# Expert feed-forward: experts sorted by token count, three of them with 64 slots, and a share of the weight splitting on GpSimd

## Chip, cores and metric

The kernel runs on one core of a Trainium2 chip. The metric is the device time of one execution in microseconds (us); the number quoted is the median over the runs.

## What is computed

The reference is a two-layer encoder trunk on 256 tokens of width 1024. The change touches the last stage, the second layer's channel mixer, in which each token goes to the best two of eight experts:

```python
logits = h @ router_w + router_b
top_v, top_i = lax.top_k(logits, 2)
probs = softmax(top_v)
for e in range(8):
    out += combine[..., e:e+1] * ((silu(h @ w1[e]) * (h @ w3[e])) @ w2[e])
```

Here `w1[e]` and `w3[e]` are 1024 x 3584 and `w2[e]` is 3584 x 1024, all in fp32: 44 MB an expert, 352 MB in all.

## The kernel before

**Precision.** TensorE multiplies in a reduced-precision fp32 form (`F32R`), so each operand is split into a high and a low part: ScalarE writes `hi` as a copy in that form, VectorE then writes `lo = x - hi` (`split`, lines 271 to 273). A product takes three matmuls, `hi*hi`, `hi*lo` and `lo*hi` (`mm3`, lines 275 to 280).

**Tokens.** Every expert has 128 slots. `tokens` makes, for two experts at a time, a 0/1 matrix `sel` that puts the chosen tokens in the slots, gathers their `h` by matmul, and splits it into the parts in `hg` (in one of three places, named `hhi`, `hlo` or `hg` in the trace). `selT` and `wsl` bring the result back with the router's weight. A second pass over all experts runs only if an expert has over 128 tokens.

**Blocks.** An expert's 3584 hidden columns are cut into seven blocks of 512 (`f`), so there are 56 blocks. In a block, `up` makes `ph` for `w1` and for `w3`: eight chunks of the 1024 inputs, three matmuls each with the token part stationary and 512 weight columns moving, so 48 matmuls. Then ScalarE takes Silu of the first (line 1739) and VectorE multiplies by the second and by `wsl` (line 1740, tile `ea`). `turned` transposes `ea` by four TensorE instructions into `aT` and splits it into `eahi` and `ealo`; `down` adds 24 matmuls into the two accumulators `py`. `up` of a block stands ahead of `down` of the block before it.

**Weights.** A block reads six tiles of 1 MiB (two each of `w1`, `w3`, `w2`) into 14 raw buffers: ten named `er`, and the places `ey`, `hg` and `x`, of which four are filled at the start and two stay in use. SyncE issues all of them in order (line 163), each when its buffer is free. `Stream.splits` turns each tile into two pieces of 1024 columns, `eh` (ScalarE) and `el` (VectorE), in four buffers each, asked for three pieces ahead of their use. Each engine's order comes from a scheduler that lays the program out when it is built.

Of the kernel before, what the change touches and what calls it, by code (L numbers as in the profile page):

```python
# [35 lines left out]
T = 256  # L36
# [9 lines left out]
CAP = 128  # L46
# [4 lines left out]
def _consts():  # L51
# [24 lines left out]
    late["slots"] = np.broadcast_to(p, (128, 128))  # L76
    out = []
# [52 lines left out]
class Stream:  # L130
# [19 lines left out]
    def load(self, upto):  # L150
        while self.loaded < min(upto, len(self.tiles)):
            t = self.tiles[self.loaded]
            k, m = self.loaded - self.bufs, len(self.more)
            if k >= m:
                k = (k - m) % (self.bufs + self.keep) - self.bufs + m - self.keep
            if k >= m - self.keep or 0 <= k == self.loaded - self.bufs:
                raw = self.more[k]()
            else:
                raw = self.pool.tile([128, self.raw], F32, name=self.name + "r", tag=self.name + "r", bufs=self.bufs)
            dst = raw[:, :t[1]]  # L160
            if len(t[0].shape) == 3:
                dst = dst.rearrange("p (a b) -> p a b", a=t[0].shape[1])
            self.k.nc.sync.dma_start(dst, t[0])
            t[2] = raw
            self.loaded += 1
# [6 lines left out]
    def splits(self, upto):  # L172
        nc = self.k.nc
        while self.split < min(upto, len(self.units)):
# [3 lines left out]
            if not whole:  # L178
# [70 lines left out]
FFN_SPAN = 6, 42  # L249
MM = 0.109  # L250


class K:
# [17 lines left out]
    def split(self, hi, lo, src):  # L271
        self.nc.scalar.activation(hi, src, AF.Copy)  # L272
        self.nc.vector.tensor_sub(lo, src, hi.bitcast(F32))  # L273
# [1257 lines left out]
    def moe(self, l):  # L1531
# [44 lines left out]
        pe.matmul(ps[:, 8:16], self.c("before"), ind[:, 1, :], start=False, stop=True)  # L1576
        pos = t28("place")
        v.tensor_copy(pos.rearrange("p a e -> p (a e)"), ps[:, :16])
        comb = t28("comb")
        mxc = mk.tile([1, 1], I32, name="mxc")  # L1580

        def weights():
# [19 lines left out]
            over = mk.tile([1, 8], F32, name="over")  # L1602
            ps = self.pg("cnt")
            pe.matmul(ps[0:32, 0:8], self.c("ones")[:, 0:32], ind[:, 0, :], start=True, stop=False)
            pe.matmul(ps[0:32, 0:8], self.c("ones")[:, 0:32], ind[:, 1, :], start=False, stop=True)
            v.tensor_copy(over, ps[0:1, 0:8])
            v.tensor_reduce(mxc, over, axis=AX.X, op=OP.max)

        self.todo, self.pending, self.rsh = [], [weights], rsh
        self.comb, self.ind, self.pos, self.gate2, self.shift2 = comb, ind, pos, mod[:, 16:24], mod[:, 0:8]  # L1610
        with ExitStack() as s2:
            self.pshh = s2.enter_context(tc.tile_pool(name="pshh", bufs=2, space=PSUM))
            self.psy = s2.enter_context(tc.tile_pool(name="psy", bufs=1, space=PSUM))
            self.experts(ws)
            self.final()
            cnt = nc.values_load(mxc, min_val=0, max_val=256)
            with tc.If(cnt > CAP):
                self.pos = t28("place2")
                v.tensor_scalar(self.pos, pos, float(-CAP), None, op0=OP.add)
                self.experts(self.expert_stream())  # L1620
                self.final()
# [8 lines left out]
    def tokens(self, e0, first=False):  # L1630
# [7 lines left out]
        hg = [self.room((e0 + i) % 3).rearrange("p (i k s) -> p i k s", i=2, k=KB) for i in range(2)]  # L1638
        flat = [sel[:, tt].rearrange("p e s -> p (e s)") for tt in range(2)]

        def find(i):
            e = e0 + i
            for tt in range(2):
                v.tensor_scalar(sel[:, tt, i, :], self.c("slots"), self.pos[:, tt, e:e + 1], self.ind[:, tt, e:e + 1],
                                op0=OP.is_equal, op1=OP.mult)
# [4 lines left out]
        def norms():  # L1650
            ps = self.pg("rsb")[:, :256]
            for n in range(4):
                pe.matmul(ps, self.rsh[:, n // 2, n % 2:n % 2 + 1].to_broadcast([128, 128]), flat[n % 2], start=n == 0, stop=n == 3)
            act.activation(rsb, ps, AF.Copy)

        def gather(kb):
            if kb % 2 == 0:
                pk[0] = self.psy.tile([128, 512], F32, name="py0", tag=f"py{kb // 4}") if kb // 2 % 2 and first else self.pg("hg")
            ps, shift = pk[0][:, kb % 2 * T:kb % 2 * T + T], self.shift2[:, kb:kb + 1]
# [3 lines left out]
            v.tensor_mul(ps, ps, rsb)  # L1663
            for i in range(2):
                hi, lo, x = hg[i][:, 0, kb, :], hg[i][:, 1, kb, :], ps[:, i * 128:i * 128 + 128]
# [3 lines left out]
        def back(i):  # L1669
            e = e0 + i  # L1670
# [9 lines left out]
        self.todo += [lambda i=i: find(i) for i in range(2)]  # L1680
# [3 lines left out]
        self.todo += self.pending + [lambda i=i: back(i) for i in range(2)]  # L1684
        self.pending = []
        return hg, selT, wsl
# [7 lines left out]
    def expert_stream(self, more=(), keep=0):  # L1694
        I, nf = self.I, DFE // 512
        ws = Stream(self, self.es, "e", 2048, RAW, 1024, 4, 3, self.eq, more, keep)
        seq = [(e, f) for e in range(NE) for f in range(nf)]
        for x, y in zip(seq + [None], [None] + seq):
            if x:
                e, f = x  # L1700
                for w in ("moe_w1", "moe_w3"):
                    for k0 in (0, 4):
                        ws.add((w, e, f), I[w][e, k0 * 128:k0 * 128 + 512, f * 512:f * 512 + 512]
                               .rearrange("(k p) n -> p k n", p=128), 2048)
            if y:
                e, f = y
                for k0 in (0, 2):
                    r = f * 512 + k0 * 128
                    ap = I["moe_w2"][e, r:r + 256, :]
                    if y == seq[-1]:  # L1710
                        ap = I["moe_w2"][e, f * 512:f * 512 + 512, k0 * 256:k0 * 256 + 512]
                    ws.add(("moe_w2", e, f), ap.rearrange("(k p) n -> p k n", p=128), 2048)
        return ws

    def experts(self, ws):
# [5 lines left out]
        def up(e, f, hg, wsl, behind):  # L1721
            i = e % 2
            hps = []
            for w in ("moe_w1", "moe_w3"):
                if behind and w == "moe_w3":
                    behind[2] = turned(behind[2])
                ps = self.pshh.tile([128, 512], F32, name="ph", tag="p" + w)
                for k0 in range(0, 8, 2):
# [11 lines left out]
            v.scalar_tensor_tensor(a, a, wsl[:, i:i + 1], hps[1], op0=OP.mult, op1=OP.mult)  # L1740
            return a

        def turned(a, spare=False):
            pt = self.pg("aT")
            for k in range(4):
# [10 lines left out]
        def down(e, f, aT, py, selT, then=None):  # L1756
            ahi, alo = aT
            ends, last = f == nf - 1, e == NE - 1 and f == nf - 1
            for p in range(4):
                whi, wlo = ws.take(("moe_w2", e, f), 2)  # L1760
                for j in range(2):
                    c, kk = (p // 2, p % 2 * 2 + j) if last else (j, p)
                    self.mm3(py[c], ahi[:, kk * 128:kk * 128 + 128], alo[:, kk * 128:kk * 128 + 128],
                             whi[:, j, :], wlo[:, j, :], start=f == 0 and kk == 0, stop=ends and kk == 3)
                if then and p == 0:
                    then[2] = turned(then[2], True)
# [14 lines left out]
            elif ends:  # L1781
                for c in range(2):
                    self.todo.append(lambda c=c: self.split(y[:, 0, c, :], y[:, 1, c, :], py[c]))
# [3 lines left out]
        def back(e, kk, y, selT):  # L1787
            ps = self.pg("sct").rearrange("p (a t) -> p a t", a=2)
            for a in range(2):
                n = (kk + a) % 4 * 128  # L1790
                for j in range(2):
                    pe.matmul(ps[:, a, :], y[:, j, kk // 4, n:n + 128], selT[:, e % 2, :], start=a == 0 and j == 0, stop=j == 1,
# [12 lines left out]
        behind, nxt = None, self.tokens(0, True)  # L1805
        for e in range(NE):
            if e % 2 == 0:
                self.step(len(self.todo) if e else 0)
                hg, selT, wsl = nxt
            py = [self.psy.tile([128, 512], F32, name=f"py{c}", tag=f"py{c}") for c in range(2)]  # L1810
            for f in range(nf):
                a = up(e, f, hg, wsl, behind)
                now = [e, f, a, py, selT]
                if behind:
                    down(*behind, now if e == NE - 1 and f == nf - 1 else None)
                behind = now
                if e % 2 and f == nf - 4 and e < NE - 1:
                    nxt = self.tokens(e + 1)
        down(*behind)
# [71 lines left out]

def layout(inputs):
# [34 lines left out]
        "moe_w1": n["moe_w1"][0],  # L1927
        "moe_w3": n["moe_w3"][0],
        "moe_w2": n["moe_w2"][0],
# [19 lines left out]
```

## Time and profile before

| | |
|---|---|
| runs | 1762.18, 1765.52 (median), 1766.88 us |
| the profiled execution | 1767.88 us, of which its span (first to last instruction) 1766.1 us |
| TensorE / VectorE / ScalarE / GpSimd busy | 1686.6 / 1530.3 / 1188.5 / 6.6 us |
| granted TensorE clock, mean | 0.985 |

A "busy" TensorE is one with a matmul in flight; the ends of matmuls are modelled and they overlap, so its pace is read from the distance between starts. Times in the sections below count from the start of the span.

### The profile page before, as it was taken

The page shows a single profiled execution, that of the slowest core. Times are in us where ns is not written, and L with a number is a line of the kernel's source. Part 1 is how long each engine was busy: PE and PEld are TensorE (multiplying, and loading weights), DVE is VectorE, ACT ScalarE, POOL GpSimd, SP SyncE. Part 2 cuts the span into 40 slices and gives each one's busy share as a digit, 9 for nine tenths or more (in the row PEclk, how much of TensorE's full clock was granted, in tenths as well). Part 3 has the DMA queues.
Part 4 walks back from the last instruction along what each step waited for, and adds up shares of the span by engine and source line. Part 5 has one row for each costly group of instructions (what it writes and reads, how often), then busy time and mean ns, then how long its engine had stood idle before and what let it go on. Part 6 is the DMA issues. An engine that isn't in the chain of part 4 may idle for free.

```text
span 1766.1 us, 29679 instructions
## 1 busy us (share of the span) xinstructions
PE 1686.6 (95%) x11192; PEld 1466.2 (83%) x11192; DVE 1530.3 (87%) x2386; ACT 1188.5 (67%) x1774; POOL 6.6 (0%) x19
## 2 busy tenths in 40 slices
PE   5887999999989999899999999999999999999996
PEld 4776999999988899788888888888888888888885
DVE  7887788888869888689999998999999999999996
ACT  3645556555565655478878777777777787777775
POOL 0000000000000000000000000000000000000000
PEclk9999999999989999899999999999999999999998
DMA  8724465888733657979999999999999999999980
GB/s 283 251 92 157 153 208 190 294 288 289 249 98 125 204 185 230 345 277 366 379 344 343 355 342 366 370 351 331 352 361 372 346 365 337 347 373 367 353 304 26
DMA packets 193812, 501.93 MB, mean 284 GB/s; under 512 B 11498, under 2 KB 13162, under 8 KB 193660
## 3 DMA queue, kind: packets, MB, share of 16 engines
q1 hardware_dynamic: 192652, 498.50, 79.8%
q8 instruction: 89, 1.46, 0.3%
q10 hardware_dynamic: 720, 1.42, 0.2%
q14 instruction: 63, 0.52, 0.1%
q0 software_dynamic: 288, 0.03, 0.0%
HBM read 498.86 MB, written 1.05 MB: 283 GB/s over the span
## 4 chain that ended last, share of the span: by engine, by line
PE 77%; DVE 11%; DMA 7%; issue 3%; ACT 2%; SPq 0%; DVEq 0%; ACTq 0%
PE ph L279 10%; PE ph L278 10%; PE ph L280 10%; PE py L279 5%; PE py L280 5%; PE py L278 5%; PE pj L278 4%; PE pj L279 4%; PE pj L280 4%; DVE el L273 3%; DMA er<-in_moe_w_dram 3%; PE psh L278 2%; PE psh L279 2%; PE psh L280 2%; DVE wl L273 2%
## 5 line engine op out<-in xcount | busy, mean ns | idle before, releaser
L273 DVE TENSOR_TENSOR el<-er,eh 128x1024 fp32r<-128x1024 f32 x560 | 661.8, 1221 | 25.7 <-ACT eh L272 13.9
L272 ACT ACTIVATE eh<-er 128x1024 fp32r<-128x1024 f32 x560 | 580.9, 1059 | 104.0 <-PE ph L280 54.8
L272 ACT ACTIVATE wh<-wr 128x512 fp32r<-128x512 f32 (+1 forms) x366 | 223.0, 620 | 210.3 <-PE pj L279 61.5
L273 DVE TENSOR_TENSOR wl<-wr,wh 128x512 fp32r<-128x512 f32 (+1 forms) x366 | 242.8, 674 | 59.6 <-ACT wh L272 57.3
L278 PE MATMUL pj<-hhi,wh 128*128 128x256 f32 x704 | 206.6, 299 | 8.0 <-ACT hhi L400 7.3
L279 PE MATMUL pj<-hlo,wh 128*128 128x256 f32 x704 | 200.6, 287 | 0.6 <-DVE hlo L273 0.5
L280 PE MATMUL pj<-hhi,wl 128*128 128x256 f32 x704 | 200.5, 286 | 0.6 <-DVE wl L273 0.6
L279 PE MATMUL py<-el,eahi 128*128 128x512 f32 x440 | 175.1, 398 | 0.7
L280 PE MATMUL py<-eh,ealo 128*128 128x512 f32 x440 | 171.8, 391 | 0.0
L278 PEld LDWEIGHTS pj<-hhi,wh 128*128 128x128 f32 x704 | 134.5, 194 | 16.2 <-ACT hhi L400 8.9
L278 PE MATMUL py<-eh,eahi 128*128 128x512 f32 x440 | 146.4, 390 | 0.0
L279 PEld LDWEIGHTS pj<-hlo,wh 128*128 128x128 f32 x704 | 136.4, 194 | 2.8 <-issue 1.1
L280 PEld LDWEIGHTS pj<-hhi,wl 128*128 128x128 f32 x704 | 136.4, 194 | 1.9 <-DVE wl L273 1.1
L273 DVE TENSOR_TENSOR el<-x,eh 128x1024 fp32r<-128x1024 f32 x108 | 128.2, 1221 | 8.0 <-ACT eh L272 6.1
L278 PE MATMUL ph<-eh,hhi 128*128 128x512 f32 x336 | 133.6, 398 | 0.5 <-ACT hhi L1666 0.5
L278 PE MATMUL ph<-eh,hlo 128*128 128x512 f32 x336 | 133.2, 396 | 0.0
L279 PE MATMUL ph<-el,hhi 128*128 128x512 f32 x336 | 133.0, 396 | 0.1
L279 PE MATMUL ph<-el,hlo 128*128 128x512 f32 x336 | 132.9, 396 | 0.0
L280 PE MATMUL ph<-eh,hhi 128*128 128x512 f32 x336 | 131.9, 393 | 0.0
L280 PE MATMUL ph<-eh,hlo 128*128 128x512 f32 x336 | 131.8, 392 | 0.0
L272 ACT ACTIVATE eh<-x 128x1024 fp32r<-128x1024 f32 x108 | 111.6, 1057 | 14.2 <-PE ph L280 12.8
L279 PEld LDWEIGHTS py<-el,eahi 128*128 128x128 f32 x440 | 82.7, 188 | 19.8 <-DVE el L273 3.2
(413 smaller groups left out, 3389.7 us busy)
## 6 DMA issues: line engine op xcount, KB each, us to landing
er<-in_moe_w_dram SPq DMA_DIRECT2D x280, 1024.0 KB, 7.1
x<-in_moe_w_dram SPq DMA_DIRECT2D x54, 1024.0 KB, 7.1
wr<-in_ada_w_dram SPq DMA_DIRECT2D x64, 512.0 KB, 4.4
wr<-in_w_in_dram SPq DMA_DIRECT2D x52, 512.0 KB, 4.3
wr<-in_ffn_up_dram SPq DMA_DIRECT2D x44, 512.0 KB, 4.4
aw<-in_ada_w_dram SPq DMA_DIRECT2D x32, 512.0 KB, 4.8
wr<-in_ffn_w_dram SPq DMA_DIRECT2D x22, 512.0 KB, 4.7
wr<-in_w_o_dram SPq DMA_DIRECT2D x16, 512.0 KB, 4.6
```

What stands on the lines that cost most here:

```text
L272: self.nc.scalar.activation(hi, src, AF.Copy)
L273: self.nc.vector.tensor_sub(lo, src, hi.bitcast(F32))
L278: mm(out, whi, xhi, start=start, stop=False, skip_group_check=True)
L279: mm(out, whi, xlo, start=False, stop=False, skip_group_check=True)
L280: mm(out, wlo, xhi, start=False, stop=stop, skip_group_check=True)
```

## The change

1. **Order.** `arranged` counts the tokens of each expert on the chip, ranks the experts by it and sets which expert is worked on at which place: expert 0 first, then by turns one of the three with the fewest tokens (places 1, 3, 5, the set `SMALL`) and one of the others. The weights of places 1 to 7 are read from an address that SyncE takes from a register (`order`).
2. **Small experts.** They have 64 slots. The high part of `h` fills columns 0 to 63 of the stationary operand, the low part columns 64 to 127. A product then takes two matmuls, by `whi` and by `wlo`, and rows 0 to 63 and 64 to 127 of `ph` are added later: both `ph` are copied to SBUF (`ea`, `eb`), and eight matmuls by the constant `sum2` add and transpose them at once. Silu and the product follow on 128x256 (`ez`), and both parts go into one stationary operand for `down` (`ealo`), with `wsl` applied at the end (`weighed`).
3. **GpSimd.** For the small experts' weights, VectorE writes the first 640 columns of a piece of `el` and GpSimd the last 384 (`POOLED`).
4. **Weights in memory.** They are laid out so that each partition's 2048 elements of a tile lie together; before, they were four runs of 512 (`w1`, `w3`) or two of 1024 (`w2`).
5. **Groups.** `tokens` runs for places (0), (1, 2), (3, 4), (5, 6), (7) in place of pairs. A second pass over all experts runs if one has more tokens than its slots.

```diff
+SMALL = (1, 3, 5)
+PLACE = (0, 5, 1, 6, 2, 7, 3, 4)
+GROUPS = ((0,), (1, 2), (3, 4), (5, 6), (7,))
+POOLED = 384
...
+                elif self.aside(r):
+                    m = n - POOLED
+                    self.k.split(hi[:, :n], lo[:, :m], src, m)
+                    self.k.nc.gpsimd.tensor_sub(lo[:, m:n], src[:, m:], hi[:, m:n].bitcast(F32))
...
     def expert_stream(...):
-                        ws.add((w, e, f), I[w][e, k0 * 128:k0 * 128 + 512, f * 512:f * 512 + 512]
-                               .rearrange("(k p) n -> p k n", p=128), 2048)
+                at = lambda i=i: I[w][bass.ds(self.order(e), 1), f, i].rearrange("a p n -> (a p) n")
+                ws.add((w, e, f), at if e and sorted_ else I[w][e, f, i], 2048)
...
     up:
-                        self.mm3(ps, hg[i][:, 0, kb, :], hg[i][:, 1, kb, :], whi[:, k, :], wlo[:, k, :],
-                                 start=kb == 0, stop=kb == 7)
+                        if e in small:
+                            pe.matmul(ps, x[:, kb, :], whi[:, k, :], start=kb == 0, stop=False, skip_group_check=True)
+                            pe.matmul(ps, x[:, kb, :], wlo[:, k, :], start=False, stop=kb == 7, skip_group_check=True)
+                        else:
+                            self.mm3(ps, hi[:, kb, :], lo[:, kb, :], whi[:, k, :], wlo[:, k, :], start=kb == 0, stop=kb == 7)
...
+            if e in small:
+                b = self.ex.tile([128, 512], F32R, name="eb", tag="eahi", bufs=1).bitcast(F32)
+                v.tensor_copy(a, hps[0])
+                v.tensor_copy(b, hps[1])
+                return a, b
...
     turned:
+            if e in small:
+                for i in range(2):
+                    for k in range(4):
+                        o = i * 256 + k * 64
+                        pe.matmul(pt[:, o:o + 64], a[i][:, k * 128:k * 128 + 128], self.c("sum2"), start=True, stop=True)
+                z = self.work.tile([128, T], F32, name="ez", tag="sq", bufs=3)
+                tc.keep_in_program_order(act.activation(z, pt[:, :T], AF.Silu))
+                v.tensor_mul(z, z, pt[:, T:])
...
+                v.tensor_copy(t4[:, :, 0, :], z)
+                v.tensor_sub(t4[:, :, 1, :], z, t4[:, :, 0, :].bitcast(F32))
...
     down:
+                    if e in small:
+                        pe.matmul(py[c], aT[:, sl], whi[:, j, :], start=first, stop=False, skip_group_check=True)
+                        pe.matmul(py[c], aT[:, sl], wlo[:, j, :], start=False, stop=stop, skip_group_check=True)
...
-        behind, nxt = None, self.tokens(0, True)
+        behind, hg = None, self.tokens(GROUPS[0], small, True)
```

`arranged` is some 26 VectorE instructions on tiles of at most 64 columns and two matmuls.

**TensorE, inside `up`.** Before, one piece of the weights in the middle of an expert (two of the eight chunks) and the first row of the next; `eh` and `el` are the piece's parts, and a name in brackets is the engine whose result the instruction waits for:

```order
L278 MATMUL ph<-eh,hhi 128x512 [waits Activation_49]
L279 MATMUL ph<-el,hhi 128x512 [waits DVE_49]
L280 MATMUL ph<-eh,hhi 128x512
L278 MATMUL ph<-eh,hhi 128x512
L279 MATMUL ph<-el,hhi 128x512
L280 MATMUL ph<-eh,hhi 128x512
L278 MATMUL ph<-eh,hhi 128x512 [waits Activation_49]
```

After, the same place in a small expert (`hlo` holds the tokens here):

```order
L1814 MATMUL ph<-eh,hlo 128x512 [waits Activation_49]
L1815 MATMUL ph<-el,hlo 128x512 [waits DVE_49]
L1814 MATMUL ph<-eh,hlo 128x512
L1815 MATMUL ph<-el,hlo 128x512 [waits Pool_49]
L1814 MATMUL ph<-eh,hlo 128x512 [waits Activation_49]
```

A piece goes from six matmuls to four, and the last of the four, which reads the columns past 640, waits for GpSimd.

**VectorE.** Before, around the Silu's product of one block (a gather of tokens stands between here, on `hhi`):

```order
L273 TENSOR_TENSOR el<-er,eh 128x1024 [waits PE_49]
L1667 SCALAR_TENSOR_TENSOR hhi<-hg,mod_7670,hhi 128x128 [waits Activation_49] x2
L1740 SCALAR_TENSOR_TENSOR ea<-ea,wsl,ph 128x512 [waits Activation_49]
L273 TENSOR_TENSOR el<-er,eh 128x1024 [waits DMAHW1_49,PE_49]
L273 TENSOR_TENSOR el<-er,eh 128x1024 [waits Activation_49]
```

After, in a small expert, from the copy of one `ph` to the product of the block:

```order
L290 TENSOR_TENSOR el<-er,eh 128x640 [waits DMAHW1_49,Activation_49]
L290 TENSOR_TENSOR el<-er,eh 128x640 [waits Activation_49]
L290 TENSOR_TENSOR el<-er,eh 128x640 [waits DMAHW2_49,PE_49,Activation_49]
L290 TENSOR_TENSOR el<-er,eh 128x640 [waits PE_49,Activation_49]
L290 TENSOR_TENSOR el<-er,eh 128x640 [waits DMAHW3_49,PE_49,Activation_49]
L290 TENSOR_TENSOR el<-er,eh 128x640 [waits PE_49,Activation_49]
L1825 COPY ea<-ph 128x512 [waits PE_49]
L290 TENSOR_TENSOR el<-er,eh 128x640 [waits DMAHW4_49,Activation_49]
L1843 TENSOR_TENSOR ez<-ez,aT 128x256 [waits Activation_49]
L290 TENSOR_TENSOR el<-er,eh 128x640 [waits Activation_49]
L1846 CAST ealo<-ez 128x4x64 [waits DVE_49]
L1847 TENSOR_TENSOR ealo<-ez,ealo 128x4x64 [waits DVE_49]
```

Each `el` row is 640 columns wide in place of 1024, and between them stand the copies of `ph` and the three instructions that make `ez` and `ealo`.

**GpSimd, the same stretch.** Before there is nothing here. After, a row for each piece, on the tiles that VectorE's rows read and write:

```order
L199 TENSOR_TENSOR el<-er,eh 128x384 [waits DMAHW1_49,PE_49,Activation_49]
L199 TENSOR_TENSOR el<-er,eh 128x384 [waits PE_49,Activation_49]
L199 TENSOR_TENSOR el<-er,eh 128x384 [waits DMAHW2_49,PE_49,Activation_49]
L199 TENSOR_TENSOR el<-er,eh 128x384 [waits PE_49,Activation_49]
L199 TENSOR_TENSOR el<-er,eh 128x384 [waits DMAHW3_49,PE_49,Activation_49]
```

Both engines wait for ScalarE's `eh` of the piece.

## Rows read from the trace of the kernel before

**Rows 1.** The page, whole kernel: busy time by engine; 40 slices of 44 us.

```profile
PE 1686.6 (95%) x11192; PEld 1466.2 (83%) x11192; DVE 1530.3 (87%) x2386; ACT 1188.5 (67%) x1774; POOL 6.6 (0%) x19
...
PE   5887999999989999899999999999999999999996
DVE  7887788888869888689999998999999999999996
ACT  3645556555565655478878777777777787777775
...
PEclk9999999999989999899999999999999999999998
DMA  8724465888733657979999999999999999999980
GB/s 283 251 92 157 153 208 190 294 288 289 249 98 125 204 185 230 345 277 366 379 344 343 355 342 366 370 351 331 352 361 372 346 365 337 347 373 367 353 304 26
```

**Rows 2.** The page: what ended last, by engine.

```profile
PE 77%; DVE 11%; DMA 7%; issue 3%; ACT 2%; SPq 0%; DVEq 0%; ACTq 0%
```

**Rows 3.** Line 1739, the Silu of each block: count, first and last start.

```profile
L1739 ACT ACTIVATE ea<-ph x56: 577/579/601, 771.9 to 1733.3; 128x512 f32<-128x512 f32 x56
```

**Rows 4.** TensorE in order of time, one block: start, duration (us), instruction.

```profile
1052.56 0.39 PE L278 MATMUL ph<-eh,hg 128*128 128x512 f32 x1
1052.79 0.39 PE L279 MATMUL ph<-el,hg 128*128 128x512 f32 x1
...
1068.13 0.60 PE L1746 MATMUL aT<-cst,ea 128*128 128x128 f32 x4
1068.49 0.48 PE L279 MATMUL py<-el,eahi 128*128 128x512 f32 x1
1068.80 0.40 PE L280 MATMUL py<-eh,ealo 128*128 128x512 f32 x1
...
1069.50 0.39 PE L278 MATMUL ph<-eh,hg 128*128 128x512 f32 x1
```

**Rows 5.** Windows: that block, and all blocks: busy us by engine, clock, DMA.

```profile
core 0: us, PE busy (x) PEld busy (x) DVE busy (x) ACT busy (x) POOL busy (x), PEclk, DMA share, GB/s
1052.56:1069.50 16.94, 16.94 (x77) 13.88 (x76) 15.29 (x15) 13.23 (x15) 0.00 (x0) 1.00 1.01 376
772.00:1733.00 961.00, 960.05 (x4405) 787.59 (x4404) 889.17 (x924) 746.58 (x837) 0.00 (x0) 1.00 0.96 348
```

**Rows 6.** Groups by shape, 800 to 1700 us: busy, mean ns, idle before.

```profile
L273 DVE TENSOR_TENSOR el<-er,eh 128x1024 fp32r<-128x1024 f32 x513 | 606.3, 1221 | 23.4 <-ACT eh L272 12.0 <-DMA er<-in_moe_w_dram 0.2
L272 ACT ACTIVATE eh<-er 128x1024 fp32r<-128x1024 f32 x513 | 532.4, 1059 | 95.7 <-PE ph L280 48.0 <-PE py L280 38.4 <-DVE el L273 5.4
L1740 DVE SCALAR_TENSOR_TENSOR ea<-ea,wsl,ph 128x512 f32<-128x512 f32 x51 | 37.8, 742 | 0.1
L273 DVE TENSOR_TENSOR ealo<-aT,eahi 128x512 fp32r<-128x512 f32 x51 | 35.1, 689 | 29.8 <-ACT eahi L272 29.6
L272 ACT ACTIVATE eahi<-aT 128x512 fp32r<-128x512 f32 x51 | 30.4, 596 | 76.0 <-PE py L279 44.6 <-PE aT L1746 31.4
```

**Rows 7.** SyncE's queue, 800 to 1700 us: what its issues waited for.

```profile
SPq L163 <- DVE el L273: 693.3, 280, 4.1
```

**Rows 8.** Groups by shape, whole kernel: the nearest rows for new operations.

```profile
L273 DVE TENSOR_TENSOR wl<-wr,wh 128x512 fp32r<-128x512 f32 x348 | 235.7, 687 | 59.5 <-ACT wh L272 57.3 <-PE pj L280 0.6 <-issue 0.3
L1331 DVE COPY kT<-qkT 96x512 f32<-96x512 f32 x8 | 5.5, 682 | 0.1
L1663 DVE TENSOR_TENSOR hg<-hg,rsb 128x256 f32<-128x256 f32 x28 | 11.8, 427 | 3.7 <-PE hg L1661 3.4
L1301 DVE COPY k<-krot 128x512 f32<-128x512 f32 x2 | 0.8, 421 | 0.0
L273 DVE TENSOR_TENSOR falo<-fa,fahi 128x256 fp32r<-128x256 f32 x22 | 9.2, 418 | 0.0
L1674 ACT ACTIVATE selT<-selT 128x256 fp32r<-128x256 f32 x8 | 3.1, 382 | 1.8 <-PE selT L1673 1.8
```

**Rows 9.** All of GpSimd's groups that write a tile of size.

```profile
L987 POOL MEMSET f<- 128x512 f32 x2 | 1.1, 542 | 0.0
L985 POOL MEMSET f<- 128x256 f32 x2 | 0.7, 326 | 136.5 <-PE pj L280 136.5
```

**Rows 10.** DMA, 1040 to 1120 us in slices of 2 us; transfers into `er`.

```profile
GB/s 392 383 381 329 414 408 377 382 327 331 403 375 386 387 379 318 394 298 378 372 326 372 406 307 371 385 335 286 389 371 405 407 407 391 332 397 363 367 384 420
DMA packets 12650, 29.66 MB, mean 371 GB/s; under 512 B 450, under 2 KB 450, under 8 KB 12645
...
DMA to landing us min/median/max: 3.3/7.1/15.7
L163 SPq DMA_DIRECT2D er<-in_moe_w_dram x280: 367/368/3232, 712.6 to 1709.3; - x140
```

**Rows 11.** VectorE in order of time, as the experts begin.

```profile
753.72 0.15 DVE L1596 TENSOR_TENSOR p<-d,p 128x2 f32<-128x2 f32 x1
753.79 0.34 DVE L1667 SCALAR_TENSOR_TENSOR hhi<-hg,mod,hhi 128x128 fp32r<-128x128 f32 x1
766.35 0.34 DVE L1644 TENSOR_SCALAR sel<-cst,place,ind 128x128 fp32r<-128x128 f32 x1
```

More of the change, by code (lines that the diff above doesn't have):

```diff
@@ L1600, in weights, with arranged @@
             self.dump("comb", comb)
-            over = mk.tile([1, 8], F32, name="over")
+        def arranged():
+            n, rk = mk.tile([128, 8], F32, name="n"), mk.tile([128, 8], F32, name="rk")
             ps = self.pg("cnt")
[L1604 to L1607, printed above, removed]
@@ L1609, in moe @@
[L1609 to L1610 removed]
+            pe.matmul(ps[:, 0:8], self.c("ones"), ind[:, 0, :], start=True, stop=False)
+            pe.matmul(ps[:, 0:8], self.c("ones"), ind[:, 1, :], start=False, stop=True)
+            v.tensor_copy(n, ps[:, 0:8])
+            v.tensor_copy(rk, n)
+            v.memset(rk[:, 0:1], NONE)
+            gt, eq, perm = (self.work.tile([128, T], F32, name=x, tag="sq", bufs=3)[:, :64].rearrange("p (a b) -> p a b", a=8)
+                            for x in ("gt", "eq", "perm"))
@@ new lines, in arranged @@
+            v.tensor_mul(gt[0:1], perm[0:1], self.c("index")[0:1].unsqueeze(1).to_broadcast([1, 8, 8]))
+            num = mk.tile([1, 8], F32, name="num")
+            v.tensor_reduce(num, gt[0:1], axis=AX.X, op=OP.add)
+            v.tensor_copy(self.numbers, num)
+            for x, y in ((pos, placeS), (comb, combS)):
+                for tt in range(2):
+                    v.tensor_mul(eq, perm, x[:, tt, :].unsqueeze(1).to_broadcast([128, 8, 8]))
+                    v.tensor_reduce(y[:, tt, :], eq, axis=AX.X, op=OP.add)
@@ L1628, in room, with tokens @@
         return self.hx.tile([128, KB, T], F32R, name=n, tag=n).rearrange("p k t -> p (k t)")
-    def tokens(self, e0, first=False):
+    def tokens(self, group, small, first=False):
         nc = self.nc
@@ L1678, in back @@
             v.tensor_copy(wsl[:, i:i + 1], ps[:, e:e + 1])
-        self.todo += [lambda i=i: find(i) for i in range(2)]
+        some = range(len(group))
+        self.todo += [lambda i=i: find(i) for i in some]
         self.todo += [norms] + [lambda kb=kb: gather(kb) for kb in range(KB)]
@@ L1683, in tokens @@
             self.step(len(self.todo))
-        self.todo += self.pending + [lambda i=i: back(i) for i in range(2)]
-        self.pending = []
-        return hg, selT, wsl
+        now, self.pending = self.pending, []
+        self.todo += now[:1] + [lambda i=i: back(i) for i in some] + now[1:]
+        return out
     def step(self, n=1):
@@ L1697, in expert_stream, with add, order, experts @@
         seq = [(e, f) for e in range(NE) for f in range(nf)]
+        small = []
+        def add(w, e, f):
+            for i in range(2):
+                if e in SMALL and sorted_:
+                    small.append(len(ws.tiles))
+                at = lambda i=i: I[w][bass.ds(self.order(e), 1), f, i].rearrange("a p n -> (a p) n")
+                ws.add((w, e, f), at if e and sorted_ else I[w][e, f, i], 2048)
         for x, y in zip(seq + [None], [None] + seq):
             if x:
-                e, f = x
-                for w in ("moe_w1", "moe_w3"):
-                    for k0 in (0, 4):
-                        ws.add((w, e, f), I[w][e, k0 * 128:k0 * 128 + 512, f * 512:f * 512 + 512]
-                               .rearrange("(k p) n -> p k n", p=128), 2048)
-            if y:
[L1706 to L1712, printed above, removed]
-        return ws
-    def experts(self, ws):
+                add("moe_w1", *x)
+                add("moe_w3", *x)
+            if y:
+                add("moe_w2", *y)
+        ws.aside = lambda r: r in small
+        return ws
+    def order(self, e):
+        if self.regs is None:
+            _, self.regs = self.nc.values_load_multi_w_load_instructions(
+                self.numbers[0:1, 1:8], engines=[mybir.EngineType.SP], min_val=0, max_val=NE - 1,
+                skip_runtime_bounds_check_because="each is the number of the one expert with this rank among eight")
+        return self.regs[e - 1]
+    def experts(self, ws, small):
         nc, tc, I = self.nc, self.tc, self.I
@@ L1741, in up, with turned @@
             return a
-        def turned(a, spare=False):
+        def turned(now, spare=False):
+            e, f, a = now
             pt = self.pg("aT")
+            if e in small:
+                for i in range(2):
+                    for k in range(4):
[4 more added lines that the diff above has]
+                v.tensor_mul(z, z, pt[:, T:])
+                t = self.ex.tile([128, 512], F32R, name="ealo", tag="ealo", bufs=1)
+                t4, z = t.rearrange("p (k i s) -> p k i s", k=4, i=2), z.rearrange("p (k s) -> p k s", k=4)
+                v.tensor_copy(t4[:, :, 0, :], z)
+                v.tensor_sub(t4[:, :, 1, :], z, t4[:, :, 0, :].bitcast(F32))
+                return t
@@ L1754, in turned, with down @@
             return ahi, alo
-        def down(e, f, aT, py, selT, then=None):
-            ahi, alo = aT
+        def down(e, f, aT, py, then=None):
+            selT, wsl = hg[e][3:]
             ends, last = f == nf - 1, e == NE - 1 and f == nf - 1
@@ L1791, in back @@
                 for j in range(2):
-                    pe.matmul(ps[:, a, :], y[:, j, kk // 4, n:n + 128], selT[:, e % 2, :], start=a == 0 and j == 0, stop=j == 1,
+                    pe.matmul(ps[:, a, :], y[:, j, kk // 4, n:n + 128], selT, start=a == 0 and j == 0, stop=j == 1,
                               skip_group_check=True)
@@ L1803, in back @@
                     self.square(kb, direct=4)
-        behind, nxt = None, self.tokens(0, True)
+        behind, hg = None, self.tokens(GROUPS[0], small, True)
         for e in range(NE):
-            if e % 2 == 0:
-                self.step(len(self.todo) if e else 0)
-                hg, selT, wsl = nxt
+            g = [e in x for x in GROUPS].index(True)
+            if e and e == GROUPS[g][0]:
+                self.step(len(self.todo))
             py = [self.psy.tile([128, 512], F32, name=f"py{c}", tag=f"py{c}") for c in range(2)]
             for f in range(nf):
-                a = up(e, f, hg, wsl, behind)
-                now = [e, f, a, py, selT]
+                a = up(e, f, behind)
+                now = [e, f, a]
                 if behind:
[L1815 to L1819, printed above, removed]
+                    down(*behind, pyb, now if e == NE - 1 and f == nf - 1 else None)
+                behind, pyb = now, py
+                if e == GROUPS[g][-1] and f == nf - 4 and e < NE - 1:
+                    hg = {**hg, **self.tokens(GROUPS[g + 1], small)}
+        down(*behind, pyb)
     def turn_out(self, kb):
```

133 lines of the change are left out of this document (95 added, 38 removed).

## The prediction

> **What bounds the kernel now.** I read the page first. TensorE is busy through nearly all slices from 720 us on, VectorE is close behind, and the DMA row is at 9 there as well [rows 1]; the chain that ended last is 77% TensorE [rows 2]. So three resources are candidates in the expert stage, and the page alone doesn't say which one paces it. The Silu row gives the pace: 56 blocks, the first Silu at 771.9 and the last at 1733.3 us, so 961.4 / 55 = 17.48 us a block [rows 3]. One block in the middle, in order of time, shows why. From the first matmul of `up` at 1052.56 to the same one of the next block at 1069.50 pass 16.94 us [rows 4]. Matmuls start 0.23 us apart; 72 of them at about 0.2285 are 16.45, and the four transposes take the other 0.49. In that stretch TensorE is busy for all 16.94 us at a granted clock of 1.00, VectorE for 15.29, ScalarE for 13.23 [rows 5]. TensorE sets the pace. The 17.48 - 16.94 = 0.54 us a block left over, 3.8 an expert, are the gathering and scattering of tokens.
>
> DMA looks full (share 1.01 at 376 GB/s in that block [rows 5]) but isn't what is waited for: SyncE's issues stood 693 us of 900 waiting for VectorE to free a raw buffer [rows 7]. It is demand that makes 376 GB/s: 6.29 MB in 16.94 us is 371. What DMA could do beyond it is not shown for long, only slices of 2 us at up to 420 [rows 10].
>
> **The change, engine by engine, for a block of a small expert.** There are 21 such blocks (three experts); the other 35 keep their 16.94.
> - *TensorE*: 72 matmuls become 48 of the same width: 48 x 0.2285 = 10.97. Eight small matmuls replace four transposes, at most 0.12 each by the transposes: 0.97. Sum 11.9 us.
> - *ScalarE*: the twelve `eh` stay whole: 12 x 1.059 = 12.71 [rows 6]. The Silu falls to 128x256, priced by the `selT` row, 0.38 [rows 8], and the 0.60 of `eahi` goes. Sum 13.1 us.
> - *VectorE*: 1024 columns take 1.221 and 512 take 0.687 [rows 6, 8], so 1.043 ns a column, and 640 take 0.82; twelve are 9.84. New: two copies of `ph` at 0.68 (the `kT` copy), the product at 0.43, the copy into `ealo` between nothing and the 0.42 of a copy twice as wide (I take 0.3), the subtraction 0.42 [rows 8]. Gone: `ea` 0.74 and `ealo` 0.69. Sum 12.35 us if GpSimd doesn't disturb it. Without GpSimd's share it would be 12 x 1.221 + 2.5 = 17.2, over TensorE's present pace. The saving therefore stands or falls with GpSimd.
> - *GpSimd*: no subtraction of it is in the trace. Its fills take 0.326 for 256 columns and 0.542 for 512 [rows 9], so 0.43 for 384 with a write alone. That is the lower bound; three streams one after another, 1.3, is the upper. I take 0.85, two reads one after the other with the write beside them. Twelve: 10.2 us (5.2 to 15.6).
> - *DMA*: a partition's row of a tile goes from 2 or 4 KB runs to one of 8 KB, with the bytes unchanged. The demand per block is covered below.
>
> ScalarE is then the longest, 13.1 us. A chain of four engines through four piece buffers will not run without gaps; I add 5% and take 13.8. Gain: 21 x (16.94 - 13.8) = **66 us**; at 13.1 it is 81, with GpSimd at 15.6 (the upper bound) it is 28.
>
> Smaller terms. `arranged`: 26 VectorE instructions at 0.15 to 0.35 [rows 11], some 5 us, inside the first expert, where VectorE has 16.94 - 16.08 (twelve `el`, `ea`, `ealo`) = 0.86 us a block to spare; I charge 3. The first gather now serves one expert, so eight `lo` instructions of 0.34 [rows 11] leave the start: I credit 2. `eb` shares its buffer with `eahi`, so where a big expert hands over to a small one the copy waits for the last `down`, and `ph` with it: three times about 1 us, 3. The token work of 0.54 a block stays. SyncE's extra register step per transfer is hidden: an issue takes 0.37 us [rows 10], and six of them fill 2.2 of 13.8 us. If that cover were gone it would cost the difference.
>
> Does DMA follow? In a small expert a tile is wanted every 13.8 / 6 = 2.3 us, 456 GB/s. A transfer lands in 7.1 us (median) [rows 10], so of 14 buffers some 11 are filled ahead. At the present 372 GB/s (2.82 us a tile) a small expert's 42 tiles fall 22 us short, 65 in three; 11 tiles in hand are 31 us, and a big expert refills nothing at that rate. At 397 GB/s (2.64 a tile) the shortfall is 14 for each, with 7.6 refilled in each big one, and nothing is lost. I take it that longer runs reach that.
>
> Sum against the profiled execution: 1767.9 - 66 + 3 - 2 + 3 = 1705.9. That execution is 2.4 us above the median, so **1704 us** against the runs' 1765.5. Differences under 0.3%, some 5 us, can't be told from no change.
>
> **Rivals.**
> 1. *VectorE and GpSimd can't read SBUF side by side.* Both subtractions read `er` and `eh` there, and both become ready on the same `eh`. If one has to end before the other begins, a piece costs 0.82 + 0.85 = 1.67 us, twelve 20.0, and with the copy and subtraction of `ealo` (0.7, both operands in SBUF) 20.7 a block, against 16.94: 21 x 3.8 = 79 slower, with the small terms 83, so **1849 us**. The bounds of GpSimd's price give 17.5 (GpSimd 0.43; VectorE's other 2.5 us included), or 1780, and 26.1, or 1960. Behind the matmul that waits for Pool stand all later matmuls, and ScalarE's next `eh` waits for their buffer, so nothing would hide it. It turns into a loss as soon as GpSimd takes over 0.53 us a piece. For it: the width of the VectorE rows, which already run at one column per 1.04 ns with two operands. Against it: nothing in this trace, since no GpSimd instruction stands beside a VectorE one in the stage. The Trainium skill, page "SBUF — State Buffer", section "Who interferes with whom", says that GpSimd has only the port pair that VectorE uses second, that a VectorE instruction with two SBUF inputs contends with a GpSimd one that reads SBUF, and that the pair is held for a whole instruction. By that rule the time is this rival's; no run here shows it yet. A price for GpSimd stands in the Trainium skill, "GPSIMD Engine Reference", "Elementwise — side-by-side cycle accounting": 4497 ns for 2048 columns, by which 384 would be an estimated 0.84, and the sum the same.
> 2. *The two slow each other in part.* If 0.38 of GpSimd's 0.85 stand in VectorE's way, its piece takes 1.20, a block 12 x 1.20 + 2.5 = 16.9, and only the small terms are left: **1770**, same. If 0.21 do, 1.03 and 14.9, a gain of 43 less the small terms: 1727, inside the forecast's own range.
> 3. *DMA stays at 372 GB/s*: 65 - 31 = 34 us of the gain go, **1738**.
> 4. *A small expert has more than 64 tokens.* Then all eight experts run again, near 56 x 17.48 = 979 us more. Worked out from the reference's inputs, the three have 52, 64 and 64: just no overflow, unless a near tie falls the other way.
>
> **How the numbers follow.** The forecast with rival 3 and the milder form of rival 2: 0.54 (of it 0.06 rival 3), own range 1686 to 1745. Rival 1: 0.37. Same (rival 2): 0.07. Rival 4: 0.02. Both signs hold much, since the one price that decides, how two engines share SBUF, isn't in the trace. A range of 1686 to 1866 leaves out 0.02 below, and 0.17 above, rival 1 with GpSimd at 0.9 or more and rival 4. Faster 0.54, same 0.07, slower 0.39.
>
> **What would show it.** In the profile after, `el` in the 128x640 form near 820 ns, GpSimd's 128x384 near 850, blocks of small experts 13 to 14.5 us apart, with ScalarE busy over 90% there. Rival 1 shows as `el` or GpSimd rows whose mean is near the sum of both, and as TensorE waiting for `el` by Pool and DVE; rival 3 as ScalarE waiting for DMA into `er`. The prediction is wrong if a small block takes over 16.9 us, whatever the reason.

## Result: 1826.9 us, 3.4% slower

| | median of the runs (us) | profiled execution, span (us) |
|---|---|---|
| before | 1766.05 (4 runs, 1762.2 to 1766.9) | 1766.1 |
| after | 1826.88 (4 runs, 1818.1 to 1830.1) | 1826.5 |

The ratio is 1.034, interval 1.030 to 1.038. The forecast was 1704; the time lies inside the stated range and near rival 1's 1849, on the other side of no change.

The page of the kernel after, whole kernel (busy time, slices of 46 us, the engines of the chain that ended last, two of the costliest groups):

```profile
PE 1672.5 (92%) x10976; PEld 1402.9 (77%) x10976; DVE 1578.5 (86%) x2482; ACT 1177.8 (64%) x1754; POOL 343.9 (19%) x271
...
PE   4988999999899999899978999988999888999997
...
POOL 0000000000000000000487400587200777100000
...
PE 61%; DVE 26%; issue 5%; DMA 5%; ACT 2%; DVEq 0%; POOL 0%; ACTq 0%; SPq 0%
...
L287 ACT ACTIVATE eh<-er 128x1024 fp32r<-128x1024 f32 x560 | 581.4, 1057 | 173.6 <-POOL el L199 37.8
L199 POOL TENSOR_TENSOR el<-er,eh 128x384 fp32r<-128x384 f32 x216 | 291.4, 1367 | 671.9 <-ACT eh L287 624.7
```

Against [rows 1, 2], TensorE's row falls to 7 or 8 in the slices in which GpSimd works most, those of the three small experts, and VectorE's share of the chain goes from 11% to 26%. The groups by shape, 760 to 1800 us, show what VectorE did:

```profile
L290 DVE TENSOR_TENSOR el<-er,eh 128x1024 fp32r<-128x1024 f32 x337 | 398.8, 1218 | 21.5 <-ACT eh L287 17.0
L290 DVE TENSOR_TENSOR el<-er,eh 128x640 fp32r<-128x640 f32 x216 | 283.5, 1363 | 1.0 <-ACT eh L287 0.8
```

A 640-column subtraction takes 1.363 us on the mean, longer than a 1024-column one (1.218, as in [rows 6]) in the big experts of the same run. The mean mixes two kinds: of the 216 rows, 132 last about 1.6 us and 58 last 0.8 to 0.9. In order of time, three neighbouring pieces (VectorE's rows are merged in pairs; what counts is where they start, then GpSimd's rows):

```profile
981.37 3.18 DVE L290 TENSOR_TENSOR el<-er,eh 128x640 fp32r<-128x640 f32 x2
982.92 3.19 DVE L290 TENSOR_TENSOR el<-er,eh 128x640 fp32r<-128x640 f32 x2
984.47 3.19 DVE L290 TENSOR_TENSOR el<-er,eh 128x640 fp32r<-128x640 f32 x2
...
982.76 1.11 POOL L199 TENSOR_TENSOR el<-er,eh 128x384 fp32r<-128x384 f32 x1 [0.44 <-ACT eh L287]
984.25 1.17 POOL L199 TENSOR_TENSOR el<-er,eh 128x384 fp32r<-128x384 f32 x1 [0.39 <-PE py L1869]
985.86 1.12 POOL L199 TENSOR_TENSOR el<-er,eh 128x384 fp32r<-128x384 f32 x1 [0.44 <-ACT eh L287]
```

In such a run VectorE starts a piece every 1.55 us. The quiet small blocks (those in which no tokens are gathered or scattered) are 19.6 apart (by the starts of `ez`, 1234.65, 1254.26 and 1273.88), against the 16.94 of a big block. Four rows of VectorE from the first of them, with the idle time before a row and what ended it in brackets:

```profile
1237.72 0.69 DVE L1825 COPY ea<-ph 128x512 f32<-128x512 f32 x1 [1.06 <-PE ph L1815]
1238.33 0.85 DVE L290 TENSOR_TENSOR el<-er,eh 128x640 fp32r<-128x640 f32 x1
1239.43 1.30 DVE L290 TENSOR_TENSOR el<-er,eh 128x640 fp32r<-128x640 f32 x1
1244.73 0.69 DVE L1826 COPY eb<-ph 128x512 f32<-128x512 f32 x1 [1.06 <-PE ph L1815]
```

Of that block's twelve pieces seven take about 1.63 us and one 1.30; four, next to VectorE's other work, take 0.81 to 0.86. So not every piece is held up, and 2.1 us of the block are VectorE standing idle ahead of the two copies, until TensorE's `ph` is done. Who waited for whom, 760 to 1800 us, in total, times, longest:

```profile
PEld ph L1815 <- DVE el L290: 90.8, 115, 2.9
ACT eh L287 <- POOL el L199: 48.3, 73, 1.7
PE ph L1815 <- DVE el L290: 43.0, 104, 2.5
```

TensorE waits for VectorE, and ScalarE for GpSimd to free a buffer.

The time by expert, from the first matmul on one expert's tokens to the first on the next's, read from TensorE in order of time (us; places 1, 3 and 5 are small where there are small ones; place 7 runs to the end and is left out; the experiments' columns are told of below):

| place | before | after | x3 | x1 | y1 |
|---|---|---|---|---|---|
| 0 | 117.1 | 129.3 | 125.5 | 127.7 | 129.5 |
| 1 | 126.8 | 135.7 | 120.3 | 109.8 | 105.6 |
| 2 | 121.8 | 129.7 | 127.8 | 131.7 | 128.7 |
| 3 | 127.3 | 135.1 | 121.1 | 117.9 | 107.3 |
| 4 | 121.5 | 129.7 | 127.5 | 128.8 | 128.7 |
| 5 | 127.2 | 135.2 | 121.3 | 117.9 | 107.3 |
| 6 | 121.5 | 126.3 | 126.3 | 125.3 | 125.3 |
| sum | 863.3 | 921.0 | 869.7 | 859.0 | 832.3 |

The sum grows by 57.8 of the 60.4 us between the spans.

### The profile page after: what moved, and what is told of

It reads as the page before. It is cut to its first block, busy times and chain, and to the rows that moved or that the text cites. A ratio compares the mean times of both kernels' runs of the same rounds, so it can differ in the third digit from the quotient of the medians.

```text
span 1826.5 us, 30560 instructions
## 1 busy us (share of the span) xinstructions
PE 1672.5 (92%) x10976; PEld 1402.9 (77%) x10976; DVE 1578.5 (86%) x2482; ACT 1177.8 (64%) x1754; POOL 343.9 (19%) x271
## 4 chain that ended last, share of the span: by engine, by line
PE 61%; DVE 26%; issue 5%; DMA 5%; ACT 2%; DVEq 0%; POOL 0%; ACTq 0%; SPq 0%
DVE el L290 16%; PE ph L296 5%; PE ph L297 5%; PE ph L295 5%; PE pj L295 5%; PE pj L296 4%; PE pj L297 4%; PE py L296 3%; PE py L295 3%; PE py L297 3%; DMA er<-in_moe_w_dram 2%; PE psh L295 2%; PE psh L296 2%; PE psh L297 2%; PE ph L1815 2%
## 5 line engine op out<-in xcount | busy, mean ns | idle before, releaser
L290 DVE TENSOR_TENSOR el<-er,eh 128x1024 fp32r<-128x1024 f32 (+1 forms) x560 | 689.9, 1274 | 23.0 <-ACT eh L287 18.3
L199 POOL TENSOR_TENSOR el<-er,eh 128x384 fp32r<-128x384 f32 x216 | 291.4, 1367 | 671.9 <-ACT eh L287 624.7
L290 DVE TENSOR_TENSOR el<-x,eh 128x1024 fp32r<-128x1024 f32 (+1 forms) x108 | 125.5, 1188 | 4.8 <-ACT eh L287 3.2
L296 PE MATMUL py<-el,eahi 128*128 128x512 f32 x272 | 107.8, 396 | 0.5 <-DVE el L290 0.4
L297 PE MATMUL py<-eh,ealo 128*128 128x512 f32 x272 | 106.1, 390 | 0.0
L295 PE MATMUL py<-eh,eahi 128*128 128x512 f32 x272 | 96.2, 391 | 0.0
L296 PE MATMUL psh<-xu,wh 128*128 128x258 f32 x336 | 95.3, 284 | 0.0
L295 PE MATMUL psh<-xu,wh 128*128 128x258 f32 x336 | 95.2, 283 | 0.0
L297 PE MATMUL psh<-xu,wl 128*128 128x258 f32 x336 | 94.9, 282 | 0.0
L295 PE MATMUL ph<-eh,hhi 128*128 128x512 f32 x224 | 90.8, 405 | 0.0
L296 PE MATMUL ph<-el,hlo 128*128 128x512 f32 x224 | 89.3, 398 | 0.4 <-DVE el L290 0.3
```

Source lines behind the costliest of these rows:

```text
L199: self.k.nc.gpsimd.tensor_sub(lo[:, m:n], src[:, m:], hi[:, m:n].bitcast(F32))
L295: mm(out, whi, xhi, start=start, stop=False, skip_group_check=True)
L296: mm(out, whi, xlo, start=False, stop=False, skip_group_check=True)
L297: mm(out, wlo, xhi, start=False, stop=stop, skip_group_check=True)
```

## Experiments

Theory A: GpSimd's subtraction and VectorE's, which both read two operands from SBUF, hold each other out, so that a piece costs both in turn. Rival B: the small blocks are slow for another reason in their longer chain.

**x1_no_gpsimd.** GpSimd's share goes back to VectorE.

```diff
-                elif self.aside(r):
+                elif POOLED and self.aside(r):
...
-POOLED = 384
+POOLED = 0
```

> The changed kernel with GpSimd's share taken away: VectorE writes all 1024 columns of each piece in the small experts too. Theory A (GpSimd's subtraction and VectorE's hold each other out, so a piece costs both in turn, 1.55 us in the trace of the changed kernel): a block of a small expert is then bound by VectorE, 12 x 1.22 + 2.5 = 17.2 us in place of the 19.6 seen, so some 21 x 2.4 = 50 us faster than the changed kernel, about 1777 us. Rival B (the small blocks are slow for another reason: the longer chain of copies, the register-addressed transfers, waits between four engines): taking GpSimd away puts 384 more columns on VectorE and the time stays near 1827 or rises.

Measured: 1768.1 us, ratio to the kernel before 0.999 (0.997 to 1.002). So VectorE has 384 columns more to do in each of 252 pieces, and the kernel is 59 us faster than the changed one. Rival B falls. The 1777 was too high: a quiet small block takes 15.7 us in the first small expert and settles at 16.8 in the other two, not 17.2. VectorE in order of time, in the first:

```profile
945.47 1.21 DVE L290 TENSOR_TENSOR el<-er,eh 128x1024 fp32r<-128x1024 f32 x1
946.60 1.21 DVE L290 TENSOR_TENSOR el<-x,eh 128x1024 fp32r<-128x1024 f32 x1
947.74 0.41 DVE L1843 TENSOR_TENSOR ez<-ez,aT 128x256 f32<-128x256 f32 x1
948.07 1.21 DVE L290 TENSOR_TENSOR el<-x,eh 128x1024 fp32r<-128x1024 f32 x1
949.21 0.28 DVE L1846 CAST ealo<-ez 128x256 fp32r<-128x256 f32 x1
949.41 1.21 DVE L290 TENSOR_TENSOR el<-x,eh 128x1024 fp32r<-128x1024 f32 x1
950.54 0.41 DVE L1847 TENSOR_TENSOR ealo<-ez,ealo 128x256 fp32r<-128x256 f32 x1
950.88 1.22 DVE L290 TENSOR_TENSOR el<-x,eh 128x1024 fp32r<-128x1024 f32 x1
...
955.42 0.68 DVE L1825 COPY ea<-ph 128x512 f32<-128x512 f32 x1
956.02 0.68 DVE L1826 COPY eb<-ph 128x512 f32<-128x512 f32 x1
956.62 5.75 DVE L290 TENSOR_TENSOR el<-er,eh 128x1024 fp32r<-128x1024 f32 x5
```

A row lasts 1.21, but the next starts 1.13 to 1.14 after it: VectorE's instructions overlap by some 0.08. By starts, a block is 12 x 1.135 + 0.60 + 0.60 + 0.33 + 0.20 + 0.34 = 15.7, which is what is seen. In the other two small experts VectorE stands idle once in each of the blocks of 16.8, ahead of the copy of the first `ph`, and that is the difference:

```profile
1189.69 0.69 DVE L1825 COPY ea<-ph 128x512 f32<-128x512 f32 x1 [1.07 <-PE ph L1815]
```

**x2_gpsimd_fills.** GpSimd only writes.

```diff
-                    self.k.nc.gpsimd.tensor_sub(lo[:, m:n], src[:, m:], hi[:, m:n].bitcast(F32))
+                    self.k.nc.gpsimd.memset(lo[:, m:n].bitcast(F32), 0.0)
```

> The changed kernel with GpSimd writing zeros into its 384 columns in place of subtracting, so the low part of those columns of the small experts' weights is left out of the result. GpSimd then writes SBUF and reads nothing; VectorE's part is unchanged. Theory A in its narrow form (what is shared is the reading of SBUF): VectorE's 640-column rows return to 0.81 us, a small block to ScalarE's 13.1 to 14 us, so 21 x 5.7 = 120 us faster than the changed kernel, about 1707. Theory A in a wide form (any GpSimd access holds VectorE out): a piece costs 0.81 + about 0.4, a block 14.5 + 2.5 = 17, about 1775. Rival B: no gain, since the chain is the same.

Measured: 1726.4 us, 0.977 (0.973 to 0.982). The groups by shape, VectorE's from 880 to 1700 us:

```profile
L290 DVE TENSOR_TENSOR el<-er,eh 128x640 fp32r<-128x640 f32 x216 | 168.7, 818 | 10.8 <-ACT eh L287 7.7 <-PE py L1870 1.1
L199 POOL MEMSET el<- 128x384 f32 x252 | 105.6, 419 | 808.1 <-PE py L296 589.3 <-PE ph L1815 117.0 <-PE py L1870 48.4
```

VectorE is back at 0.818, with a GpSimd fill beside each piece that takes 0.419, no more than 384 columns took alone (0.43 by interpolation of [rows 9]). The narrow form holds for the subtraction: GpSimd's writing doesn't hold it up. Its time was 19 us too low since the small blocks settle at 14.7 and not 13.9; while they do, the DMA view, 1150 to 1210 us, and the only wait of a compute engine for a transfer that the profile names from 880 to 1700 us (total, times, longest) are

```profile
DMA packets 3442, 25.08 MB, mean 418 GB/s; under 512 B 383, under 2 KB 383, under 8 KB 383
...
ACT eh L287 <- DMA er<-in_moe_w_dram: 0.8, 1, 0.8
```

A block of 14.7 us asks for 428 GB/s (6.29 MB), a little more than the 418 that were moved, but no engine is shown to have waited for it: from 1165 to 1185 us the chain that ended last is TensorE and VectorE by turns and holds no transfer. What sets 14.7 stays open.

**y2_one_sbuf_input.** GpSimd subtracts as in the change, VectorE reads one operand from SBUF.

```diff
-                    self.k.split(hi[:, :n], lo[:, :m], src, m)
+                    nc.scalar.activation(hi[:, :n], src, AF.Copy)
+                    acc = self.k.small.tile([128, 1], F32, name="one", tag="one")
+                    nc.vector.tensor_scalar(lo[:, :m], src[:, :m], 0.0, 0.0, op0=OP.mult, op1=OP.add, accum_out=acc)
```

> The changed kernel with GpSimd's subtraction as it is, and VectorE's subtraction in the small experts replaced by an instruction of the same width with one SBUF input (a multiplication by zero that also writes a sum), so the low part of 640 of 1024 columns of the small experts' weights is left out of the result. Theory A in its narrow form (the two hold each other out only where both read a second operand from SBUF): GpSimd runs beside VectorE at its own price, 0.75 to 1.0 us, VectorE near 0.8, small blocks at 14.7, bound by transfers, in all about 1727 us. Rival C (any VectorE access to SBUF and a GpSimd read hold each other out): blocks stay near 19.6 and the time at 1827.

Measured: 1742.5 us, 0.986 (0.981 to 0.991). The groups by shape (GpSimd's of the whole kernel), and two starts of VectorE in order of time:

```profile
L200 DVE TENSOR_SCALAR_CACHE_REDUCE el<-er 128x640 fp32r<-128x640 f32 x216 | 164.8, 813 | 3.5 <-PE ph L1817 1.0 <-PE py L298 0.9 <-PE ph L298 0.7
L201 POOL TENSOR_TENSOR el<-er,eh 128x384 fp32r<-128x384 f32 x216 | 215.4, 1023 | 671.0 <-ACT eh L198 582.4 <-issue 35.2 <-PE ph L1817 16.9
...
941.27 0.81 DVE L200 TENSOR_SCALAR_CACHE_REDUCE el<-er 128x640 fp32r<-128x640 f32 x1
...
942.01 0.81 DVE L200 TENSOR_SCALAR_CACHE_REDUCE el<-er 128x640 fp32r<-128x640 f32 x1
```

Neither is stretched: 0.813 and 1.023 where they were 1.363 and 1.367. Rival C falls for this instruction, and both prices are now known apart: VectorE 0.74 from start to start, GpSimd 1.02, of which it holds VectorE off for 1.55 - 0.74 = 0.81. VectorE itself would need 0.40 for those 384 columns (1.135 from start to start for 1024, as x1 shows, less the 0.74 for 640).

Two other VectorE instructions of a small block bound the condition, the subtraction and the copy that write `ealo`. They read no tile that GpSimd reads. Their rows in x1, y2 and x2 (count, then shortest, median and longest in ns; x1 has no GpSimd work there, x2 its fills):

```profile
L1847 DVE TENSOR_TENSOR ealo<-ez,ealo x21: 409/415/426, 915.3 to 1505.5; 128x256 fp32r<-128x256 f32 x21
L1849 DVE TENSOR_TENSOR ealo<-ez,ealo x21: 424/426/1187, 908.7 to 1473.3; 128x256 fp32r<-128x256 f32 x21
...
L1846 DVE CAST ealo<-ez x21: 279/284/285, 914.7 to 1505.1; 128x256 fp32r<-128x256 f32 x21
L1848 DVE CAST ealo<-ez x21: 282/294/809, 908.1 to 1473.0; 128x256 fp32r<-128x256 f32 x21
L1846 DVE CAST ealo<-ez x21: 282/285/509, 904.1 to 1459.0; 128x256 fp32r<-128x256 f32 x21
```

The subtraction, with two operands in SBUF, lasts up to 1.19 us in y2 where GpSimd's rows lie beside it, and 0.43 at most in x1, so sharing a tile isn't what collides. The copy has one operand in SBUF, and yet it lasts up to 0.81 beside GpSimd's subtraction in y2 and 0.51 beside a fill in x2, against 0.28: one SBUF operand is not enough to be left alone.

The time is 15 above the 1727 expected; the quiet blocks settle near 15.3 and not at 14.7. ScalarE's `eh` waited 40 us for GpSimd's part of `el`, whose 1.02 alone was already over the 0.75 to 1.0 allowed for; that this is the whole of the 15 isn't shown.

**y3_gpsimd_128.** A third of the share.

```diff
-POOLED = 384
+POOLED = 128
```

> The changed kernel with 128 columns of a piece on GpSimd in place of 384. Theory A (in turn, whole instructions): VectorE's part costs 0.745 + 256 x 1.043 ns = 1.01 and GpSimd's third of 0.80 or a little over, 0.3, so 1.31 us a piece against 1.157 without GpSimd and 1.55 with 384; a small block 17.6, in all about 1790 us, between x1 and the changed kernel. Rival D (a small share fits into the stretches in which VectorE reads ph, which don't collide): a piece at 1.01 to 1.1, below x1, 1750 to 1765.

Measured: 1786.0 us, 1.010 (1.005 to 1.016). VectorE's rows, 896 columns wide, start 1.26 us apart in the median of neighbours and 1.00 where GpSimd isn't in the way, so GpSimd costs 0.26 for 128 columns and 0.81 for 384: 2.0 and 2.1 ns a column. Theory A holds, at twice the 1.04 ns that VectorE needs for a column, and a share of 128 columns doesn't fit in unnoticed: rival D falls.

**x3_no_small_experts** and **x4_layout_only** take the rest of the change apart.

```diff
-SMALL = (1, 3, 5)
+SMALL = ()
```

> The changed kernel with no expert small: counting, sorting, the order of places, register-addressed transfers, the new layout and the groups of tokens stay, every expert has 128 slots and three products, GpSimd does nothing. From the experts' starts in the trace the groups (four later gathers in place of three, and dearer) cost 16 us and the start 5: theory A says 1766 + 16 + 5 = 1787 us. Rival B' (the big experts' extra time comes from GpSimd and the small experts next to them, not from the groups): 1766 within 5.

Measured: 1773.3 us, 1.003 (1.0005 to 1.006): 3 us over the 1770.1 of the kernel before on the same chip, so the 1787 of theory A fails and rival B' comes near. In the table its column sums to 6.5 more than before: a fourth gather costs about what each of three did (127.3 - 121.5). The dearer gathers in the column after (places 0, 2 and 4, 8 us together) come with the small experts beside them, not with the groups; x1 has them too, so they aren't GpSimd's either.

```diff
-                        ws.add((w, e, f), I[w][e, k0 * 128:k0 * 128 + 512, f * 512:f * 512 + 512]
-                               .rearrange("(k p) n -> p k n", p=128), 2048)
...
+                        ws.add((w, e, f), I[w][e, f, i], 2048)
```

> The kernel before with the new memory layout of the expert weights alone (8 KB in a row for each partition). DMA wasn't what the kernel before waited for, so theory A says no change, 1766 within 5 us, with transfers landing sooner (5 to 6 us in place of 7.1). Rival: DMA did hold the kernel somewhere, and this gains 5 to 20 us.

Measured: 1769.4 us, 1.001 (0.999 to 1.003), as expected, though the transfers land in 7.1 us as before [rows 10], not sooner.

**y1_copies_on_scalar.** x1 with what VectorE need not do on ScalarE.

```diff
-                v.tensor_copy(a, hps[0])
-                v.tensor_copy(b, hps[1])
+                act.activation(a, hps[0], AF.Copy)
+                act.activation(b, hps[1], AF.Copy)
...
-                v.tensor_copy(t4[:, :, 0, :], z)
+                act.activation(t4[:, :, 0, :], z, AF.Copy)
```

> x1_no_gpsimd with three VectorE instructions of a small block moved to ScalarE: the two copies of ph and the copy into ealo. In x1 the subtractions start 1.157 us apart and a quiet small block takes 15.7 (12 x 1.157 + 1.8). Theory A (VectorE paces the small blocks once GpSimd is out of the way): a block falls to 12 x 1.157 + 0.8 = 14.7, where transfers (6.29 MB at the 428 GB/s that x2 reached) also stand, so 20 to 30 us less than x1, about 1742 us, 1.5% below the kernel before. Rival: the small blocks of x1 are held by the order of the copies or by ScalarE, and the time stays at 1768.

Measured: 1733.8 us, 0.981 (0.978 to 0.985): 1.9% faster than the kernel before, 5% faster than the change, and 8 us under the 1742 expected. The window of the small expert at place 3:

```profile
1113.50:1220.80 107.30, 104.98 (x478) 75.48 (x476) 104.17 (x106) 92.54 (x113) 0.00 (x0) 1.00 0.98 394
...
PEld ph L1815 <- DVE el L290: 17.5, 40, 1.1
```

Busy times are TensorE, weight loads, VectorE, ScalarE, GpSimd; the second row is the longest wait in total from 1120 to 1215 us. VectorE (104.2 of 107.3) still paces, at 14.85 us a quiet block: TensorE's weight loads wait for its `el`.

**z1_copies_old_layout**, beside **y1_again**. The core of the edit:

```diff
-                at = lambda i=i: I[w][bass.ds(self.order(e), 1), f, i].rearrange("a p n -> (a p) n")
...
+                    x = I[w][bass.ds(self.order(e), 1) if moved else slice(e, e + 1)]
...
+                        x = x[:, i * 512:i * 512 + 512, r]
...
+                    return x.rearrange("a (k p) n -> p (a k) n", p=128)
```

> y1_copies_on_scalar with the expert weights in the memory layout of the kernel before (runs of 2 and 4 KB). In y1 the small blocks ask for 6.29 MB in 14.85 us, 424 GB/s, and the trace shows 419. Theory: the short runs reach less (in the kernel before no more than 376 GB/s over a block was ever asked for, so their ceiling isn't known); if it is 372 to 397 a small block grows to 15.8 to 16.9 once the filled buffers are used up, 10 to 35 us on y1, 1745 to 1765, and the layout then earns that much in y1 though it earned nothing by itself in x4. Rival: the short runs reach 424 too and the time stays at 1734.

> y1_copies_on_scalar once more, on the same chip as z1, for the comparison of the two: 1734 within 5 us.

Measured: 1735.2 (0.981, 0.978 to 0.984) and 1734.5 us (0.981, 0.978 to 0.984). The time is the rival's, its reason is not: in the profile of z1 the transfers stand lower, 383 GB/s from 1150 to 1210 us where y1 had 419, and still its experts take as long as y1's to 0.1 us. From 880 to 1700 us compute engines waited 2.3 us in all for weights. That seven blocks are too few to use up the filled buffers would fit this, but no run shows it. The new layout earned nothing here.

## Why the prediction was wrong

- **The step that failed** is the choice of the likeliest case: "Sum 12.35 us if GpSimd doesn't disturb it", and from it 13.8 us a small block. GpSimd does disturb it. y2 and x2 show the condition: the two subtractions collide because both read operands from SBUF and VectorE reads two; GpSimd's fill, or y2's VectorE instruction with one SBUF input, runs beside the other undisturbed. The Trainium skill, "SBUF — State Buffer", section "Who interferes with whom", says so of VectorE instructions outside its two-port modes and says that a copy can enter these and then collides with GpSimd. These runs agree on the subtractions, and the copy into `ealo`, stretched to 0.81 and 0.51, fits; whether it was in such a mode no run shows. The prediction quoted the rule and gave its result 0.37.
- **Rival 1** had the mechanism and 20.7 us a block; 19.6 was seen in quiet blocks. Its GpSimd price (0.85) was right for what VectorE loses (0.81), and VectorE's own 0.82 from durations is 0.74 from start to start. That the sums come so near is in part luck: eight of a quiet block's twelve pieces are held up and not all, and VectorE's 2.1 us of waiting for `ph` stands in no term. Nor do its bounds go together: 20.7 and 26.1 count 0.7 us of VectorE's other work, 17.5 counts 2.5, so by that sum a price of 0.43 is a loss already, and not only one over 0.53. The small experts are 15.4, 14.0 and 13.9 us longer than the big ones in their places in x3, 43.3 in all; rival 1 had 79 for them.
- **"The saving therefore stands or falls with GpSimd"** was wrong too: 17.2 without GpSimd was a sum of durations, and x1 shows 15.7 to 16.8, under the 16.94 of a big block, though it saves nothing in all. With three copies moved to ScalarE as well it is y1's 14.85, and that saves 1.9%. The rows had shown that durations overlap: the twelve `el`, `ea` and `ealo` of a block sum to 16.08, and VectorE was busy for 15.29 in it [rows 5].
- **Small terms.** The sums by expert split into 43.3 for the small ones, 8 for their neighbours and 6.5 for the groups. The groups weren't priced (only `arranged`, 3, and the first gather, -2).
- **DMA** (rival 3) was not the cause, as forecast: 418 to 419 GB/s were reached. The longer runs, on which the prediction let this rest, weren't needed for the time: z1 ran at 383 with the old layout and took no longer than y1.
- **ScalarE at 13.1** is no floor either, but a sum of durations: in x2 one quiet block of the first small expert takes 12.8 us (by the starts of `ez`, 930.97 and 943.75). Most settle at 14.7, for a reason that stays open.

## What to carry to other kernels

Before elementwise work is shared between VectorE and GpSimd, look at where each operand lies: where both subtracted tiles in SBUF, the shares added up instead of overlapping, and the 384 columns cost VectorE 0.81 us to spare it 0.40. Price a saturated engine by the distance between starts, not by the durations of its rows. What paid here was moving VectorE's copies, two from PSUM and one from SBUF, to ScalarE, as y1 did.

## What was not expected of the hardware

VectorE's 1024-column subtraction lasts 1.21 us, and the next one starts 1.135 after it; for 640 columns 0.81 and 0.74. GpSimd's 384-column subtraction lasts 1.02 us alone but holds VectorE off for 0.81. A copy of VectorE's with one SBUF operand was held up even by a fill (0.51 us against 0.28). And identical programs differ ahead of the experts: the experts of y1 and y1_again take 832.3 and 832.4 us, while their first matmul stands at 749.7 in one and 761.4 in the other, nearly all of the 13.0 us between their spans.
